# A hybrid encoder layer in split fp32: order of the loads at the turn to the down projection, a fixed list of down units, stores on another engine's queue

## The chip, the cores and the metric

The kernel runs on one NeuronCore of a Trainium2 chip. The metric is the device time of one execution in microseconds. Three runs of the kernel before took 2485.86 to 2487.36 us, with a median of 2487.01. One execution was taken by the hardware profiler; its own time was 2484.48 us, its span from the first instruction to the last 2482.8 us, with a mean granted TensorE clock of 0.987. All times of instructions below come from that one execution, counted from the start of its span.

## What is computed

One layer of a streaming encoder, in fp32, on 512 prompt frames and 64 sample frames (576 together), width D = 2048:

```python
def hybrid_layer(x, k_past, v_past, conv_past, g_norm1, w_in, g_q, g_k, conv_w,
                 g_attn_out, g_conv_out, w_out, g_norm2, w_gate, w_up, w_down):
    hn = rmsnorm(x, g_norm1)
    proj = hn @ w_in
    ...
    mix = jnp.concatenate([rmsnorm(o_attn, g_attn_out), rmsnorm(o_conv, g_conv_out)], axis=-1)
    x = x + mix @ w_out
    h2 = rmsnorm(x, g_norm2)
    x = x + (jax.nn.silu(h2 @ w_gate) * (h2 @ w_up)) @ w_down
    return x, k, v, new_conv
```

Eight heads of stick-breaking attention and eight groups of a short gated convolution make `mix`. The change touches only the last part, the feed-forward block: gate and up are 2048 x 5632, down is 5632 x 2048.

## The kernel before

**Split fp32.** Each operand is a pair: `hi`, the value rounded to fp32r by a ScalarE cast (L221), and `lo`, the rest, by a VectorE subtraction (L222). A product is three matmuls per 128 rows of depth, hi x hi, lo x hi and hi x lo, each over 288 columns, half of the frames (`step` L211, `multiply` L1067 to L1074).

**Stages.** In order: x is loaded, normed and turned; the input projection and the heads and groups run (to about 930 us with the output projection); the first 256 hidden channels ("pair 0" of 22 pairs) go through `wide`, the plain form, until 982 us; then 21 pairs, each a gate and an up unit, until 1927 us; then the down phase to the end. A spawned worker, `frame_sums`, makes the sums of frame halves (`tsum`) that the units need, beside the matmuls of `wide`.

**Units.** A unit computes a 256-wide block of outputs for all frames by seven products in place of eight, a Strassen-like form. The products are named 1, 2, 6, 7, 5, 3, 4 in the order in which a unit runs them, and (n, p) is product p of unit n. Operands of weights are sums and differences of the unit's two weight blocks: `prepare` makes them on VectorE and splits them two products ahead (`AHEAD = 2`), into four rotating buffers `whl`. Product 6 is the first that needs the unit's second block (the sum `s` at L1057). A gate or up unit has a depth of 8 steps of 256, so each product is 24 matmuls. The order of TensorE's products is a list written out by hand, `order`. It interleaves neighbours: the next unit's product 1 comes between a unit's products 5 and 3. The other engines' order follows from a scheduler.

**Forms.** The down phase needs seven combinations of each pair's hidden values. As the up unit ends, `put_forms` makes them, and `put_form` (L924 to L928) splits each one into a tile "hl" of two buffers and stores it, 288 KB, to DRAM. A store has to be done before the buffer's next cast.

**Down phase.** A unit (d, a, b) adds the pairs a to b - 1 to output block d, of eight. Its products are b - a steps deep, three matmuls each. `down_windows` computes the list of 35 units: 2, 3, 4, 5, 6 pairs at first, then mostly 6, with units of 1 to 3 at the end. A pair's seven forms come back as one 2016 KB slot; there are seven slots (`load_pair`, L1142 to L1146), three of which lie over the tiles of normed frames, and four, with everything else of the pool `dpool`, over the frame sums `tsum`. A slot is reloaded when all eight blocks have used its pair: `calls` says after which unit. For each unit the residual block x2, 576 KB, is loaded into one of two buffers (L1131), VectorE adds the products to it (L1140), and it is stored again (L1135) or, when the block is complete, turned and put out as y (L1161, L1162, L1168).

**Queues.** All these loads and stores are issued by SyncE (SP), which goes through its list in order: an instruction that waits holds up all behind it. At the turn the seven slots come first, each waiting for the tile that it lies over, then x2 of the first down unit, with the last pair's form stores between them.

Of the kernel before, what the change touches and what calls it, by code (L numbers as in the profile page):

```python
# [10 lines left out]
F32 = mybir.dt.float32  # L11
# [5 lines left out]
P = 128  # L17
# [3 lines left out]
HALF = T // 2  # L21
# [14 lines left out]
NFP = NFF // 2  # L36
DC = D // 256
SLOTS = 7
WINDOW = 6
FORMS = 7  # L40


def down_windows():

    done, units, calls, gone, turn = [0] * DC, [], [], {}, 0  # L50
    while min(done) < NFP:
        u = len(units)
        d = turn % DC
        turn += 1
        end = 0
        while end < NFP and (end < SLOTS or gone.get(end - SLOTS, u) <= u - 2):
            end += 1
        end = min(end, done[d] + WINDOW, u + 2 if u < DC else NFP)
        if end == done[d]:
            continue  # L60
        units.append((d, done[d], end))
        done[d] = end
        calls.append([p + SLOTS for p in range(min(done)) if p not in gone and p + SLOTS < NFP])
        for p in range(min(done)):
            gone.setdefault(p, u)
    return units, calls


class Pipeline:
# [28 lines left out]
def tile_hybrid_stream_step(  # L98
# [6 lines left out]
    nc = tc.nc  # L105
# [14 lines left out]
    tmp = ctx.enter_context(tc.tile_pool(name="tmp", bufs=2, side="left"))  # L120
    acon = tc.alloc_tile_pool(name="acon", bufs=1, side="left")
    xt_dram = tc.dram_tile([KD, P, T], F32, name="xt_dram")
    x2_dram = tc.dram_tile([KD, P, T], F32, name="x2_dram")
    hid_dram = tc.dram_tile([NFP, P, FORMS, 2, HALF], F32, name="hid_dram")
# [22 lines left out]

    UNITS = [(kind, fp, 0, NP) for fp in range(1, NFP) for kind in ("gate", "up")]
    NGU = len(UNITS)
    windows, calls = down_windows()  # L150
    UNITS += [("down", d, a, b - a) for d, a, b in windows]
    first_block = len(specs)
    for kind, i, a, n in UNITS:
        w = {"gate": w_gate, "up": w_up, "down": w_down}[kind]
# [54 lines left out]
    pipe = Pipeline()  # L209
# [10 lines left out]
    def split(hi, lo, src, lo_eng=None):  # L220
        nc.scalar.copy(out=hi, in_=src)  # L221
        (lo_eng or nc.vector).tensor_tensor(out=lo, in0=src, in1=hi.bitcast(F32), op=ALU.subtract)  # L222
# [141 lines left out]
    with tc.manual_schedule(engines={mybir.EngineType.Activation, mybir.EngineType.DVE, mybir.EngineType.SP}):  # L364
# [26 lines left out]
        for kt in range(KD + LAG):  # L391
# [19 lines left out]
            if kt in (14, 16):  # L411
                a = (kt - 14) * 512
# [424 lines left out]
    h2pool = tc.alloc_tile_pool(name="h2pool", bufs=1, reuse_waits="tile", side="left")  # L837
# [4 lines left out]
    b12pool = tc.alloc_tile_pool(name="b12pool", bufs=1, reuse_waits="tile", side="left")  # L842
# [44 lines left out]
    turn = [0]  # L887
# [9 lines left out]
    def frame_sums():  # L897

        for j in range(NP):
            ev, od = x2(2 * j), x2(2 * j + 1)  # L900
            ge, go = col("g2", 2 * j), col("g2", 2 * j + 1)
            pool, tag = (tpool, f"t{j}") if j < 4 else (ypool, f"y{j - 4}")
            b11 = tmp.tile([P, HALF], F32, tag="ms", name="b11", bufs=1)
            b22 = tmp.tile([P, HALF], F32, tag="t", name="b22", bufs=1)
            nc.scalar.activation(out=b11, in_=ev[:, :HALF], func=AF.Copy, scale=ge)
            nc.scalar.activation(out=b22, in_=od[:, HALF:], func=AF.Copy, scale=go)
            t1 = h2pool.tile([P, HALF], F32, bufs=2, tag="hx", name="t1")
            t2 = tmp.tile([P, HALF], F32, tag="sq", name="t2")
            t3 = h2pool.tile([P, HALF], F32, bufs=2, tag="hx", name="t3")
            t4 = tmp.tile([P, HALF], F32, tag="sq", name="t4")  # L910
            nc.vector.scalar_tensor_tensor(out=t1, in0=ev[:, HALF:], scalar=ge, in1=b11, op0=ALU.mult, op1=ALU.subtract)
            nc.vector.tensor_tensor(out=t2, in0=b22, in1=t1, op=ALU.subtract)
            nc.vector.scalar_tensor_tensor(out=t3, in0=ev[:, HALF:], scalar=ge, in1=b22, op0=ALU.mult, op1=ALU.subtract)
            nc.vector.scalar_tensor_tensor(out=t4, in0=od[:, :HALF], scalar=go, in1=t2, op0=ALU.mult, op1=ALU.subtract)
            tt = pool.tile([P, 2, 4, HALF], F32R, tag=tag, name=f"tsum{j}")
            for n, t in enumerate((t1, t2, t3, t4)):
                split(tt[:, 0, n, :], tt[:, 1, n, :], t)
            tsum.append(tt)
            yield 9

# [3 lines left out]
    def put_form(fp, n, src):  # L924

        t = tmp.tile([P, 2, HALF], F32R, tag="hl", name="form")
        split(t[:, 0], t[:, 1], src)
        nc.sync.dma_start(out=hid_dram[fp][:, n - 1], in_=t.bitcast(F32))  # L928

    def put_forms(fp, c, i):  # L930

# [42 lines left out]
    def wide(kind, hold=None):  # L974

        pss = {}
        for kk in range(2):
# [13 lines left out]
            if hold and kk == 0:  # L991
                hold()

    pipe.spawn(frame_sums(), 28)
    wide("gate", row_scale2)
    load_weight()
    wide("up")
# [21 lines left out]
        return [(tsum[j][:, 0, q, :], tsum[j][:, 1, q, :]) for j in range(m)]  # L1019

    NU = len(UNITS)
    order = [(0, 1), (0, 2), (0, 6), (0, 7), (0, 5)]
    for n in range(NU):
        if n == NGU - 1:

            order += [(n, 3), (n, 4), (n + 1, 1), (n + 1, 2), (n + 1, 6), (n + 1, 7), (n + 1, 5)]
            continue
        if n + 1 < NU:
            order.append((n + 1, 1))
        if n == NGU - 2:  # L1030
            order += [(n, 3), (n + 1, 2), (n + 1, 6), (n + 1, 7), (n + 1, 5), (n, 4)]
            continue
        order += [(n, 3), (n, 4)]
        if n + 1 < NU:
            order += [(n + 1, p_) for p_ in (2, 6, 7, 5)]
# [89 lines left out]
    xt2 = {}  # L1125
    down = {}

    def load_x2(n):
        d = UNITS[n][1]
        xt2[n] = down["pool"].tile([P, 2, T], F32, tag="x2", name=f"x2_{n}", bufs=2)  # L1130
        nc.sync.dma_start(out=xt2[n], in_=x2_dram[2 * d : 2 * d + 2].rearrange("k p t -> p k t"))  # L1131

    def store_x2(n):
        d = UNITS[n][1]
        nc.sync.dma_start(out=x2_dram[2 * d : 2 * d + 2].rearrange("k p t -> p k t"), in_=xt2.pop(n))  # L1135

    def add(n, c, i, src):
        a, b = HALVES[i]
# [3 lines left out]
    def load_pair(p):  # L1142
        tag = ("h2ah", "h2al", "b22", "s3", "s4", "s5", "s6")[p % SLOTS]
        pool = h2pool if p % SLOTS < 3 else down["pool"]
        slots[p] = pool.tile([P, FORMS, 2, HALF], F32R, tag=tag, name=f"slot{p}")
        nc.sync.dma_start(out=slots[p].bitcast(F32), in_=hid_dram[p])  # L1146
# [28 lines left out]
    for k_, (n, p_) in enumerate(order):  # L1175
        if p_ == 1:
            while len(raws) < min(first_block + 2 * (n + 1) + 2, len(specs)):
                load_weight()
        if (n, p_) == (NGU, 1):
            tpool.release()  # L1180
            ypool.release()
            down["pool"] = tc.alloc_tile_pool(name="dpool", bufs=1, reuse_waits="tile", side="right")
            for p in range(SLOTS):
                load_pair(p)
        if n >= NGU and p_ == 1:
            load_x2(n)
        if k_ + AHEAD < len(order):
            prepare(*order[k_ + AHEAD])
        run(n, p_)
        if n >= NGU and p_ == 4:  # L1190
            for p in calls[n - NGU]:
                load_pair(p)
# [35 lines left out]
```

## Time and profile before

| what | us |
|---|---|
| median of three runs | 2487.01 |
| profiled execution | 2484.48 |
| its span | 2482.8 |
| TensorE busy | 2422.5 |
| VectorE busy | 1759.9 |
| ScalarE busy | 1071.3 |
| GpSimd (POOL) busy | 118.3 |

How to read the profile: PE is TensorE's matmuls, PEld its weight loads beside them, DVE is VectorE, ACT ScalarE, POOL GpSimd; SPq, ACTq and PEq are what an engine's sequencer does, DMA issues above all. In a row of the timeline stand the start, the duration, the engine, the line of the kernel, the operation, and its tiles (out<-in, buffer numbers left out), with the number of instructions merged into the row. In brackets at the end is the idle time of the engine before the row, and what ended it. The granted clock (PEclk) is a share of full speed. The issue of a DMA is short; "to landing" is the time from there until the data has arrived. Tiles have short names there: the residual block x2 is x.

### The profile page before, as it was taken

How to read it: one execution, taken by the hardware profiler on the slowest of the kernel's cores; microseconds unless marked ns; L12 is line 12 of the kernel's file. 1: busy time of each engine (PE TensorE's matmuls, PEld its weight loads, DVE VectorE, ACT ScalarE, POOL GpSimd, SP SyncE). 2: the span in 40 equal slices, each digit the busy share in tenths (PEclk: the TensorE clock that was granted, in tenths of full speed). 3: DMA queues.
4: the chain of work that ended last, by engine and by line, in shares of the span. 5: the costliest groups of instructions: out<-in, count | busy, mean ns of one | idle time of the engine just before them, and what ended most of it. 6: DMA issues, size and time to landing. Idle time of an engine off the chain costs nothing.

```text
span 2482.8 us, 43866 instructions
## 1 busy us (share of the span) xinstructions
PE 2422.5 (98%) x18121; PEld 2411.9 (97%) x18121; DVE 1759.9 (71%) x2770; ACT 1071.3 (43%) x1869; POOL 118.3 (5%) x211
## 2 busy tenths in 40 slices
PE   8999999999999999999999999999999599999998
PEld 8999999999999999999999999999999599999998
DVE  7766666353335458888888888888887587777787
ACT  6655555231132345444444444444444343433443
POOL 2111010110020120000000000000000000000000
PEclk9999999999999999999999999999999799999998
DMA  8233322233242333435444454444454958778674
GB/s 268 82 93 87 91 76 84 81 88 86 78 155 84 105 123 122 135 118 159 145 143 138 126 155 150 137 137 133 150 155 156 321 173 276 246 254 264 214 215 133
DMA packets 465984, 368.33 MB, mean 148 GB/s; under 512 B 9790, under 2 KB 420024, under 8 KB 462968
## 3 DMA queue, kind: packets, MB, share of 16 engines
q1 hardware_dynamic: 464504, 365.01, 47.2%
q8 instruction: 142, 2.33, 0.4%
q10 hardware_dynamic: 1280, 0.53, 0.1%
q14 instruction: 58, 0.48, 0.1%
HBM read 285.26 MB, written 80.23 MB: 147 GB/s over the span
## 4 chain that ended last, share of the span: by engine, by line
PE 92%; DVE 3%; DMA 3%; ACT 1%; issue 0%; SPq 0%; ACTq 0%; DVEq 0%
PE psy L1071 32%; PE pj L213 23%; PE psw L1071 16%; PE pjo L213 8%; PE psx L1071 8%; DMA slot<-hid_dram 1%; DMA x<-x_dram 1%; DVE xlo L347 1%; PE z L551 1%; PE pw L986 1%; PE po L617 1%; DVE tsum L222 0%; PE os L647 0%; PE zs L577 0%; PE pot L1160 0%
## 5 line engine op out<-in xcount | busy, mean ns | idle before, releaser
L222 DVE TENSOR_TENSOR whl<-raw,whl 128x1024 fp32r<-128x1024 f32 (+5 forms) x462 | 481.2, 1042 | 109.4 <-ACT whl L221 108.3
L221 ACT CAST whl<-raw 128x1024 fp32r<-128x1024 f32 (+5 forms) x462 | 418.7, 907 | 299.4 <-issue 111.7
L213 PE MATMUL pj<-xhi,whi 128*128 128x288 f32 x1504 | 451.0, 300 | 0.0
L213 PE MATMUL pj<-xlo,whi 128*128 128x288 f32 x1504 | 445.2, 296 | 2.2 <-DVE xlo L347 2.2
L213 PE MATMUL pj<-xhi,wlo 128*128 128x288 f32 x1504 | 444.9, 296 | 0.0
L1071 PE MATMUL psy<-slot,whl 128*128 128x288 f32 x2112 | 299.6, 298 | 12.5 <-DMA slot<-hid_dram 9.8
L1071 PEld LDWEIGHTS psy<-slot,whl 128*128 128x128 f32 x2112 | 287.9, 190 | 14.3 <-DMA slot<-hid_dram 10.5
L1071 PE MATMUL psy<-tsum,whl 128*128 128x288 f32 x2016 | 283.8, 297 | 6.6 <-ACT whl L221 5.7
L213 PEld LDWEIGHTS pj<-xlo,whi 128*128 128x128 f32 x1504 | 284.5, 189 | 2.4 <-DVE xlo L347 2.4
L213 PEld LDWEIGHTS pj<-xhi,wlo 128*128 128x128 f32 x1504 | 284.9, 189 | 0.5 <-DVE wlo L177 0.2
L213 PEld LDWEIGHTS pj<-xhi,whi 128*128 128x128 f32 x1504 | 284.9, 189 | 0.3
L1071 PEld LDWEIGHTS psy<-tsum,whl 128*128 128x128 f32 x2016 | 274.4, 190 | 7.2 <-ACT whl L221 5.9
L1071 PE MATMUL psw<-tsum,whl 128*128 128x288 f32 x2016 | 280.9, 295 | 0.0
L1071 PEld LDWEIGHTS psw<-tsum,whl 128*128 128x128 f32 x2016 | 271.8, 189 | 0.0
L176 ACT CAST whi<-raw 128x1024 fp32r<-128x1024 f32 (+1 forms) x138 | 140.0, 1030 | 234.0 <-PE pj L213 95.8
L1081 ACT COPY part<-psy 128x288 f32<-128x288 f32 x231 | 92.1, 399 | 323.7 <-PE psy L1071 303.6
L1071 PE MATMUL psw<-slot,whl 128*128 128x288 f32 x1056 | 155.6, 299 | 25.0 <-DVE x L1140 25.0
L177 DVE TENSOR_TENSOR wlo<-raw,whi 128x1024 fp32r<-128x1024 f32 (+1 forms) x132 | 160.2, 1227 | 23.4 <-ACT whi L176 21.9
L1071 PEld LDWEIGHTS psw<-slot,whl 128*128 128x128 f32 x1056 | 146.6, 192 | 25.3 <-DVE x L1140 25.2
L1071 PE MATMUL psy<-b,whl 128*128 128x288 f32 x1008 | 140.2, 295 | 0.0
L1071 PEld LDWEIGHTS psy<-b,whl 128*128 128x128 f32 x1008 | 135.9, 188 | 0.0
L1071 PE MATMUL psy<-h2ah,whl 128*128 128x288 f32 x672 | 135.6, 296 | 0.0
(329 smaller groups left out, 3985.9 us busy)
## 6 DMA issues: line engine op xcount, KB each, us to landing
raw<-in_w_in_dram SPq DMA_DIRECT2D x47, 1024.0 KB, 5.5
raw<-in_w_gate_dram SPq DMA_DIRECT2D x44, 1024.0 KB, 6.2
raw<-in_w_up_dram SPq DMA_DIRECT2D x44, 1024.0 KB, 6.5
hid_dram<-form SPq DMA_DIRECT2D x154, 288.0 KB, 3.2
slot<-hid_dram SPq DMA_DIRECT2D x22, 2016.0 KB, 9.5
raw<-in_w_down_dram SPq DMA_DIRECT2D x40, 768.0 KB, 5.9
x<-x_dram SPq DMA_DIRECT2D x35, 576.0 KB, 4.6
raw<-in_w_out_dram SPq DMA_DIRECT2D x16, 1024.0 KB, 5.3
```

The source lines that it names most:

```text
L176: nc.scalar.copy(out=hi[:, a:b], in_=raw[:, a:b])
L177: lo_eng.tensor_tensor(out=lo[:, a:b], in0=raw[:, a:b], in1=hi[:, a:b].bitcast(F32), op=ALU.subtract)
L213: mm(ps, w_[:, k, csl], x_[:, k, a:b], start=(k == 0 and n == 0), stop=(k == nk - 1 and n == 2))
L221: nc.scalar.copy(out=hi, in_=src)
L222: (lo_eng or nc.vector).tensor_tensor(out=lo, in0=src, in1=hi.bitcast(F32), op=ALU.subtract)
L347: nc.vector.scalar_tensor_tensor(out=xlo[:, kt, :], in0=st, scalar=g1c[:, kt : kt + 1], in1=xhi[:, kt, :].bitcast(F32), op0=ALU.mult, op1= ...
L551: mm(zb[i], a_[:, kk], b_[:, q0:TP], start=(n == 0), stop=False, skip_group_check=True)
L617: mm(po[:, i * P : 512], a_[:, i, :], b_[:, : 512 - i * P], stop=(i == 0 and n == 2), **kw)
L986: mm(pss[j, i], w_[:, k, j * P : (j + 1) * P], x_, start=(kk == 0 and k == 0 and n == 0), stop=(kk == 1 and k == 7 and n == 2))
L1071: mm(ps, whl[:, w_, j, :], x_, start=(start and j == 0 and q == 0), stop=(j == len(xs_) - 1 and q == 2), skip_group_check=True)
L1081: nc.scalar.copy(out=t, in_=st["y"])
```

## The change

- The first units' order: product 1 of the second unit comes before product 6 of the first, and the second unit's product 2 before the first's 3.
- The down units are a fixed list, `DOWN`: 36 units of 3 to 7 pairs. The number of pairs and blocks, and so of matmuls, stays.
- At the turn only three slots are issued ahead of the first residual block; slot 3 follows it, and slots 4 to 6 follow one per unit, behind that unit's residual block.
- The stores of forms and of residual blocks are issued by GpSimd.
- `frame_sums` writes the four sums into one tile and splits them with one cast and one subtraction of 1152 columns; its worker starts after 20 ticks in place of 28.

In the changed program SP has 403 instructions (495 before), and POOL 154 form stores and 28 stores of residual blocks.

```diff
-WINDOW = 6
+DOWN = (
+    (0, 0, 3), (1, 0, 4), (2, 0, 4), (3, 0, 4), (4, 0, 5), (0, 3, 7), (5, 0, 4), (6, 0, 5), (7, 0, 6),
+    (1, 4, 7), (2, 4, 8), (3, 4, 8), (4, 5, 10), (5, 4, 9), (6, 5, 10), (0, 7, 12), (7, 6, 11), (1, 7, 12),
+    (5, 9, 14), (2, 8, 15), (3, 8, 15), (4, 10, 15), (6, 10, 15), (7, 11, 16), (0, 12, 17), (1, 12, 15),
+    (5, 14, 19), (1, 15, 19), (2, 15, 22), (1, 19, 22), (3, 15, 22), (4, 15, 22), (5, 19, 22), (6, 15, 22),
+    (0, 17, 22), (7, 16, 22),
+)
+def down_calls():
+    done, calls, gone = [0] * DC, [], 0
+    for d, a, b in DOWN:
+        assert done[d] == a and b <= gone + SLOTS
+        done[d] = b
+        calls.append([p + SLOTS for p in range(gone, min(done)) if p + SLOTS < NFP])
+        gone = min(done)
...
-            t1 = h2pool.tile([P, HALF], F32, bufs=2, tag="hx", name="t1")
...
+            t = b12pool.tile([P, 4, HALF], F32, tag="ht", name="t")
+            t1, t2, t3, t4 = (t[:, n] for n in range(4))
...
-            for n, t in enumerate((t1, t2, t3, t4)):
-                split(tt[:, 0, n, :], tt[:, 1, n, :], t)
+            split(tt[:, 0], tt[:, 1], t)
...
-        nc.sync.dma_start(out=hid_dram[fp][:, n - 1], in_=t.bitcast(F32))
+        nc.gpsimd.dma_start(out=hid_dram[fp][:, n - 1], in_=t.bitcast(F32))
...
-    pipe.spawn(frame_sums(), 28)
+    pipe.spawn(frame_sums(), 20)
...
-    order = [(0, 1), (0, 2), (0, 6), (0, 7), (0, 5)]
-    for n in range(NU):
+    order = [(0, 1), (0, 2), (1, 1), (0, 6), (0, 7), (0, 5), (1, 2), (0, 3), (0, 4), (1, 6), (1, 7), (1, 5)]
+    for n in range(1, NU):
...
-        nc.sync.dma_start(out=x2_dram[2 * d : 2 * d + 2].rearrange("k p t -> p k t"), in_=xt2.pop(n))
+        nc.gpsimd.dma_start(out=x2_dram[2 * d : 2 * d + 2].rearrange("k p t -> p k t"), in_=xt2.pop(n))
...
-            for p in range(SLOTS):
+            for p in range(3):
                 load_pair(p)
-        if n >= NGU and p_ == 1:
             load_x2(n)
+            load_pair(3)
+        if n > NGU and p_ == 1:
+            load_x2(n)
+            if n < NGU + SLOTS - 3:
+                load_pair(n - NGU + 3)
```

More of the change, by code (lines that the diff above doesn't have):

```diff
@@ L38 @@
 SLOTS = 7
-WINDOW = 6
 FORMS = 7
[L43 to L66, printed above, removed]
+DOWN = (
[5 rows of a table added]
+)
[6 more added lines that the diff above has]
+        gone = min(done)
+    assert gone == NFP
+    return calls
 class Pipeline:
@@ L149, in tile_hybrid_stream_step @@
     NGU = len(UNITS)
-    windows, calls = down_windows()
-    UNITS += [("down", d, a, b - a) for d, a, b in windows]
+    calls = down_calls()
+    UNITS += [("down", d, a, b - a) for d, a, b in DOWN]
     first_block = len(specs)
@@ L906, in frame_sums @@
             nc.scalar.activation(out=b22, in_=od[:, HALF:], func=AF.Copy, scale=go)
-            t1 = h2pool.tile([P, HALF], F32, bufs=2, tag="hx", name="t1")
-            t2 = tmp.tile([P, HALF], F32, tag="sq", name="t2")
-            t3 = h2pool.tile([P, HALF], F32, bufs=2, tag="hx", name="t3")
-            t4 = tmp.tile([P, HALF], F32, tag="sq", name="t4")
+            t = b12pool.tile([P, 4, HALF], F32, tag="ht", name="t")
+            t1, t2, t3, t4 = (t[:, n] for n in range(4))
             nc.vector.scalar_tensor_tensor(out=t1, in0=ev[:, HALF:], scalar=ge, in1=b11, op0=ALU.mult, op1=ALU.subtract)
```

## The prediction

> **What bounds the kernel now.** I read the page's totals first, then the share of each engine in the chain that ended last, then windows of TensorE to find where it stands, and then the timeline of each such place.
>
> ```profile
> span 2482.8 us, 43866 instructions
> ...
> PE 2422.5 (98%) x18121; PEld 2411.9 (97%) x18121; DVE 1759.9 (71%) x2770; ACT 1071.3 (43%) x1869; POOL 118.3 (5%) x211
> ...
> PE 92%; DVE 3%; DMA 3%; ACT 1%; issue 0%; SPq 0%; ACTq 0%; DVEq 0%
> ```
>
> TensorE is busy for 98% of the span. The change touches no matmul, so it can win only what TensorE now loses: idle time, and time at a lower clock. The windows show where that is (columns: window, us, PE busy with its matmuls, granted clock, DMA share, GB/s).
>
> ```profile
> 980.00:1000.00 20.00, 13.37 (x84) 0.78 0.69 209
> 996.00:1000.00 4.00, 3.93 (x16) 0.50 0.38 147
> 1920.00:1940.00 20.00, 13.50 (x100) 0.92 1.01 388
> 1940.00:1960.00 20.00, 0.00 (x0) 0.50 0.99 382
> 1960.00:1980.00 20.00, 19.05 (x132) 0.90 0.72 228
> 1980.00:2000.00 20.00, 20.00 (x152) 1.00 0.76 221
> 2060.00:2080.00 20.00, 16.11 (x121) 1.00 0.95 321
> 2080.00:2100.00 20.00, 20.00 (x142) 0.91 0.92 286
> 2220.00:2240.00 20.00, 16.61 (x106) 0.83 0.98 330
> 2460.00:2480.00 20.00, 14.95 (x81) 0.73 0.37 97
> ```
>
> A full window holds 152 matmuls, so one matmul of 288 columns costs 20/152 = 0.1316 us. Missing matmuls times 0.1316 is the loss, and that counts idle time and low clock together. By that measure:
> - The step into the first gate/up units (980 to 1000) misses 68: 8.9 us.
> - The turn to the down phase (1920 to 1980) misses 52 + 152 + 20 = 224: 29.5 us.
> - Three later windows of the down phase miss 31 + 10 + 46 = 87: 11.4 us.
> - The tail, 2460 to the end at 2482.8, holds some 81 matmuls in 22.8 us: 22.8 - 10.7 = 12.1 us.
>
> Together 62 us. Each part of the change aims at one of the four.
>
> **The first units.**
>
> ```profile
> 968.02 0.37 SPq L183 DMA_DIRECT2D raw<-in_w_up_dram  x1
> ...
> 982.30 0.37 SPq L183 DMA_DIRECT2D raw<-in_w_gate_dram  x1
> ...
> 988.65 1.23 DVE L1057 TENSOR_TENSOR s<-raw 128x1024 f32<-128x1024 f32 x1 [3.25 <-DMA raw<-in_w_gate_dram]
> ...
> 994.51 0.61 PE L1071 MATMUL psy<-tsum,whl 128*128 128x288 f32 x1 [5.68 <-ACT whl L221]
> ```
>
> Product (0,6) needs sums of the unit's second weight block, and that load is issued at 982.30 and read at 988.65. TensorE stands 5.68 us before it, and the window 996 to 1000 then runs at a clock of 0.50. The changed order puts (1,1) there: 8 pairs x 3 = 24 matmuls = 3.2 us of work whose block was loaded at 968.02. It moves work and adds none, so it covers 3.2 us; the idle stretch left is about 2.5 us, and a part of the low-clock stretch goes too. What is late next is (0,6)'s own cast on ScalarE: in the changed order seven casts of pair 0's forms stand before it (five now), over two buffers. With a store that takes L us to free its buffer the seventh ends near 984 + 3L, at L = 3.5 near 994.5, and the operand near 995.6; (0,6) then starts at about the time it starts now, with 3.2 us done already. I take a loss of 5.4 in place of 8.9: **-3.5 us**. Ends: -7 (nothing late) and +3 (L at the 7.4 of a row below).
>
> The frames' sums become one 1152-wide cast and one subtraction in place of four each: the same elements, fewer starts.
>
> ```profile
> L221 ACT CAST tsum<-t x32: 415/428/435, 934.5 to 978.1; 128x288 fp32r<-128x288 f32 x32
> ```
>
> The last cast ends at 978 and the first reader of tsum is the matmul at 994.51. That cover of some 14 us hides it: **0**. If the one group buffer serialised the groups, it would have to lose those 14 us before anybody waited.
>
> **The turn.**
>
> ```profile
> 1924.10 0.32 SPq L1146 DMA_DIRECT2D slot<-hid_dram  x1
> ...
> 1936.76 1.16 SPq L928 DMA_DIRECT2D hid_dram<-form  x2
> 1938.01 0.41 SPq L1146 DMA_DIRECT2D slot<-hid_dram  x1
> 1942.40 0.32 SPq L928 DMA_DIRECT2D hid_dram<-form  x1
> 1942.82 0.89 SPq L1146 DMA_DIRECT2D slot<-hid_dram  x2
> 1943.80 0.44 SPq L1131 DMA_DIRECT2D x<-x_dram  x1
> ...
> 1923.90 3.32 PE L1071 MATMUL psw<-tsum,whl 128*128 128x288 f32 x24
> ...
> 1934.51 1.47 PE L1071 MATMUL psy<-slot,whl 128*128 128x288 f32 x9 [2.48 <-DMA slot<-hid_dram]
> ...
> 1960.95 1.33 PE L1071 MATMUL psw<-slot,whl 128*128 128x288 f32 x4 [24.98 <-DVE x L1140]
> ```
>
> SP issues in order. The residual tile x of unit 0 stands behind seven slots and behind form stores that themselves wait for ScalarE, so it goes out only at 1943.80, and then shares the engines with 2016 KB slots at 382 GB/s. VectorE can't add, the accumulators stay full, and TensorE stands 24.98 us.
>
> After the change the form stores are POOL's, and SP goes slot 0, 1, 2, x(0), slot 3. Slot 2 is still freed when (up,3) ends, at 1924.10.
>
> ```profile
> DMA to landing us min/median/max: 10.4/10.4/10.4
> ```
>
> That is slot 2's landing, and 1924.10 + 10.4 = 1934.5, which the matmul at 1934.51 confirms. Unit 0 now has three pairs and so can't start on two as now: TensorE idles from the end of the last up product, 1923.90 + 3.32 = 1927.2, to 1934.5, 7.3 us; then come about 4 us at half clock. In the window 996 to 1000, 16 matmuls stand where 30 would fit, which is 1.9 us lost. Loss 9.2. Behind it: x(0), issued near 1927.3, and slot 3 right after it, since both lie over sums whose last reader ends there. Slot 3 at 10.4 and some sharing lands by about 1941.4, and it is wanted by unit 1 after the first five products of unit 0, 5 x 9 = 45 matmuls = 5.9 us plus 1.9 behind 1934.5, at 1942.3. So it holds by one microsecond. Slots 4 to 6 go out one per unit, each unit being 7 products of 4 pairs = 84 matmuls = 11 us, against 9.5 per slot. The loss goes from 29.5 to 9.2: **-20.3 us** (ends -22.2, if the clock doesn't drop, and -12, the first rival).
>
> **The fixed list.**
>
> ```profile
> hid_dram<-form SPq DMA_DIRECT2D x154, 288.0 KB, 3.2
> slot<-hid_dram SPq DMA_DIRECT2D x22, 2016.0 KB, 9.5
> ```
>
> ```profile
> 2078.89 3.68 PE L1071 MATMUL psy<-slot,whl 128*128 128x288 f32 x18 [3.88 <-DMA slot<-hid_dram]
> ```
>
> Later losses are waits for slots, as at 2078.89. A slot is reloaded when the last of the eight output blocks has used its pair. I counted for each reloaded pair the products between that and the first unit that reads it, at 3 x 0.1316 = 0.395 us per pair. Pair 0 is free at the first of six steps of the last product of (7,0,6), and pair 7 is read in the fourth step of (2,4,8): 5 + 4 products x 3 + 3 = 20 steps lie between, 7.9 us against 9.5 landing. All other pairs have 10.4 us or more. So 1.6 us of wait are left, and about 0.4 for units of three pairs, whose seven products of 1.2 us leave VectorE little room. Loss 2 in place of 11.4: **-9.4 us** (ends -11.4 and -4, the latter if landings stretch to 12 or 13 us next to weight loads).
>
> **The tail.**
>
> ```profile
> 2474.61 0.73 PE psw L1071 x3
> ...
> 2479.24 0.56 DVE ob L1161
> ```
>
> The last product ends at 2475.3 and the span at 2482.8. That part (adds, transposes, copy, the last store) is unchanged. Before it, one- and two-pair units leave gaps; the last two units are now 5 and 6 pairs. I take 7 of the 12.1 us as staying: **-5 us** (ends -6.6 and -2).
>
> **The stores on POOL.** 154 form stores and 28 x stores leave SP. The trace has no POOL DMA, so its cost is bounded by the nearest rows. The cast of the third form waits for the store of the first:
>
> ```profile
> 1395.55 0.45 DVE L222 TENSOR_TENSOR form<-ut,form 128x288 fp32r<-128x288 f32 x1
> ...
> 1398.22 0.43 ACT L221 CAST form<-ut 128x288 fp32r<-128x288 f32 x1 [0.57 <-DMA hid_dram<-form]
> 1398.53 0.45 DVE L222 TENSOR_TENSOR form<-ux,form 128x288 fp32r<-128x288 f32 x1
> ...
> 1402.54 0.40 ACT L1081 COPY part<-psy 128x288 f32<-128x288 f32 x1 [0.47 <-PE psy L1071]
> ```
>
> ```profile
> L865 POOL TENSOR_TENSOR acc<-acc,sq 128x288 f32<-128x288 f32 x30 | 26.3, 875 | 175.9 <-ACT sq L864 175.9
> ```
>
> ```profile
> x_dram<-x SPq DMA_DIRECT2D x27, 576.0 KB, 7.4
> ```
>
> From the end of the subtraction (1396.00) to the cast (1398.22) is L = 2.2 us on SP, the lower end. The upper end is 7.4, an x store behind the loads of its ring. I take 3.5: 2.2, plus one POOL instruction of 0.875, near the 3.2 of form stores as a whole. Behind a cast that waits are ScalarE's next operand cast and its copy of a partial product, and TensorE waits for that copy only when the accumulator is wanted again:
>
> ```profile
> 1405.70 9.58 PE psy L1071 x72
> ```
>
> The third form's subtraction ends at 1398.98; the cast that waits for its store (0.43), and the copy of (n,6)'s partial product that follows it in the changed order (0.40), have to be done by 1405.70, when the next product into that accumulator starts, so the cast by 1404.8. So the cover per pair is 5.8 us: at L = 3.5 the 21 pairs cost **0**; above 5.8 each us costs 21 pairs + 3 (first units) + 2 (turn) = 26 us.
>
> The Trainium skill, page "DMA: Bandwidth & Descriptors", section "Anatomy of one DMA", gives a POOL-issued DMA 2.0 us plus bytes/436e3; by it a form store would take an estimated 2.7 us, and the sum would come out the same, with 0.8 us x 3 = 2.4 us less at the first units. No run here shows it yet.
>
> **The sum.** -3.5 - 20.3 + 0 - 9.4 - 5 + 0 = -38 us. The profiled execution took 2484.5 us (span 2482.8), so 2446.3 on its basis. The median of the runs is 2487.0, 2.5 above, so 2448.8; I forecast **2449 us**.
>
> **Rivals.**
> 1. *Transfers bound the turn and the list anyway.* For: the DMA share is 1.01 and 0.99 from 1920 to 1960. If slots 0 to 3 and x(0) shared one stream, slot 2 would come 5 us later (2016 KB at 382 GB/s is 5.4 us), slot 3 and x(0) too, and the turn would lose 17.5 (-12), the list win 4, and the rest stay: -3.5 - 12 - 4 - 5 = -24.5, **2462 us**. Against: slot 2 is issued before slot 3 and x(0) may go, at 1927, so little else is in flight.
> 2. *POOL's stores gate ScalarE: slower.* Place: the two form buffers, in each of 21 pairs. It decides from L = 5.8, and eats the gain of 38 at 5.8 + 38/26 = 7.3. Near the 7.4 of x stores, with the casts queued for two stores in a row (a form store behind another on POOL), L reaches 7.7: 26 x 1.9 = 49, **2498 us**. For: POOL executes the stores one after another, and four come in about 5 us. Against: POOL is busy 5%, and its ring holds no loads. The Trainium skill, page "SBUF — State Buffer", box "The 'DVE blocks DMA' trap" in "SBUF: two separate sides", speaks for this rival: GpSimd writes a DMA's descriptors and is locked out while VectorE runs in a two-port mode. Its section "Who interferes with whom" says that tensor_tensor has no such mode, and VectorE's rows here are those; no run here shows the lock.
> 3. *The change does not do what it says*: loads still wait on something other than SP's order. Then the turn keeps 29.5 and the list changes both ways: **2485 us**. Against: slot 4 and x went out right behind form stores on SP (1936.76 to 1938.01, 1942.40 to 1943.80), so the order did hold them.
>
> **How the numbers follow.** Forecast 0.58 (own range 2438 to 2460), rival 1 with halves of it 0.24 (to 2474), rival 2 0.12, rival 3 0.04, below 2438 0.02. The range 2438 to 2474 leaves out 0.18. A difference of 0.2%, 5 us, is about what a measurement can tell from none. Faster by more: 0.85 (forecast, rival 1, below, a little of 3); within: 0.03; slower: 0.12 (rival 2).
>
> **What would show it.** TensorE's longest wait (24.98 for x) should be gone, and one of about 7 us for slot 2 stand in its place. The window of the first units should miss some 40 matmuls, not 68. Slot waits later in the down phase should sum to about 2 us. ScalarE's form casts may wait longer for stores, while TensorE shows no wait for part copies. The prediction is wrong if POOL's form stores land after more than 5.8 us, if slot 2 or slot 3 lands after more than 12, or if units of three pairs leave TensorE waiting for VectorE's adds each time.

## The result, and the profile after

The changed kernel takes 2492.31 us (median of 20 runs, 2486.31 to 2498.02), the kernel before 2486.89 us (20 runs, 2481.87 to 2491.35): a ratio of 1.0023 with a 95% interval of 1.0016 to 1.0031. It is slower by some 5 us, where 38 us of gain were forecast. The profiled execution took 2492.62 us.

The page of the changed kernel, totals and the chain that ended last:

```profile
span 2490.9 us, 43942 instructions
...
PE 2427.2 (97%) x18121; PEld 2414.4 (97%) x18121; DVE 1757.3 (71%) x2764; ACT 1069.6 (43%) x1855; POOL 222.2 (9%) x393
...
PE 53%; issue 35%; DMA 4%; POOL 3%; DVE 3%; ACT 1%; SPq 0%; POOLq 0%; ACTq 0%; DVEq 0%
```

TensorE executes the same 18121 matmuls. The share of "issue" in the chain is new. It is time for which the chain shows no releaser, and TensorE's busy time says that it is mostly no loss. The windows tell more. These are TensorE's windows of the changed kernel, with the columns and at the places of those before:

```profile
980.00:1000.00 20.00, 12.73 (x93) 0.88 0.65 206
996.00:1000.00 4.00, 0.61 (x1) 0.50 0.38 147
1920.00:1940.00 20.00, 12.18 (x80) 0.84 0.98 382
1940.00:1960.00 20.00, 14.81 (x92) 0.73 0.63 225
1960.00:1980.00 20.00, 20.00 (x152) 1.00 1.01 340
2060.00:2080.00 20.00, 11.44 (x84) 0.84 1.01 409
2080.00:2100.00 20.00, 17.77 (x114) 0.82 0.74 234
2220.00:2240.00 20.00, 20.00 (x153) 1.00 0.52 155
```

The empty window of the turn (1940 to 1960) now holds 92 matmuls. But 2060 to 2100 misses 106 where it missed 41, and more such places follow. Two of them are 2160 to 2200 and 2320 to 2360:

```profile
2160.00:2180.00 20.00, 18.77 (x137) 1.00 0.84 265
2180.00:2200.00 20.00, 15.96 (x117) 1.00 0.86 297
2320.00:2340.00 20.00, 13.89 (x103) 0.91 1.05 382
2340.00:2360.00 20.00, 19.28 (x124) 0.83 0.48 152
```

They ran at full rate in the kernel before; its second and third of these windows:

```profile
2180.00:2200.00 20.00, 20.00 (x153) 1.00 0.54 162
2320.00:2340.00 20.00, 20.00 (x153) 1.00 0.59 173
```

What TensorE waited for in the changed kernel (engine, line and releaser; us in total, times, longest):

```profile
PE psy L1064 <- ACT whl L217: 16.9, 2, 10.5
PE psy L1064 <- DMA slot<-hid_dram: 14.2, 3, 7.0
PE psy L1064 <- ACT part L1074: 6.7, 3, 6.0
PE psy L1064 <- DVE whl L218: 6.5, 6, 3.2
```

The wait of 25 us for the residual block is gone, as forecast. In its place stand weight operands (whl), slots, and a partial product's copy.

**A measure for all runs.** The loss of a stretch is its length less its matmuls at 20/152.7 = 0.131 us. It has a floor: from 1100 to 1900 in the kernel before TensorE is busy throughout at a clock of 1.00 with 6040 matmuls, and the measure still gives 8.9 us. So only differences between kernels are read. The stretch 1980 to 2360 is counted in one piece here; the expectations counted it in six windows, which take some matmuls twice at the edges (36.8 where it is 38.0 here, 14.5 where it is 16.0). All values come from one profiled execution each, so small differences say little. Each ratio is to runs of the kernel before in the same rounds, with medians of 2486.65 to 2488.34. "End" is 2360 to the last instruction.

| kernel | median us | ratio to before, 95% | first units 980–1020 | turn 1920–1980 | list 1980–2360 | end |
|---|---|---|---|---|---|---|
| before | 2486.89 | | 9.9 | 29.6 | 16.0 | 14.9 |
| changed | 2492.31 | 1.0016–1.0031 | 10.7 | 17.8 | 38.0 | 11.8 |
| e1_old_list | 2470.22 | 0.9918–0.9947 | 10.3 | 16.5 | 14.4 | 14.6 |
| e2_stores_sp | 2476.91 | 0.9937–0.9970 | 7.3 | 14.2 | 31.9 | 11.5 |
| e3_turn_seven_first | 2501.49 | 1.0038–1.0068 | 11.2 | 27.5 | 35.6 | 11.7 |
| e4_spread | 2488.38 | 0.9995–1.0014 | 11.1 | 15.5 | 33.4 | 12.0 |
| e5_forms_sp | 2484.08 | 0.9979–0.9999 | 7.5 | 14.6 | 38.5 | 11.5 |
| e6_old_list_sp | 2470.49 | 0.9916–0.9946 | 6.9 | 15.5 | 17.3 | 14.6 |
| e7_before_turn | 2473.19 | 0.9928–0.9958 | 9.6 | 17.0 | 17.8 | 14.5 |
| e8_hl3 | 2488.82 | 0.9997–1.0015 | 10.7 | 10.9 | 41.1 | 14.3 |
| e9_old_sums | 2493.54 | 1.0010–1.0034 | 12.5 | 17.4 | 38.4 | 11.6 |
| e10_part_reload | 2466.88 | 0.9902–0.9932 | 10.3 | 16.9 | 14.0 | 9.1 |
| e11_before_list | 2493.37 | 1.0011–1.0031 | 10.0 | 29.1 | 28.4 | 12.4 |
| e12_best | 2481.17 | 0.9966–0.9985 | 6.9 | 13.1 | 16.5 | 27.7 |
| e13_room | 2469.91 | 0.9910–0.9949 | 6.7 | 16.5 | 16.9 | 15.3 |
| e14_x2_pool | 2486.35 | 0.9985–1.0004 | 10.9 | 15.5 | 31.7 | 15.3 |
| e15_tail | 2466.24 | 0.9906–0.9936 | 6.6 | 16.3 | 16.5 | 15.6 |

The changed kernel's row against the one before: +0.8, -11.8, +22.0 and -3.1, together +7.9, against 8.1 between the spans. Most of the lost gain is in the list.

**At the first burst.** The timeline of the changed kernel on SP, ScalarE and TensorE, from the ninth down unit (7, 0, 6):

```profile
2054.01 2.13 SPq L1139 DMA_DIRECT2D slot<-hid_dram  x4
2059.92 16.41 SPq L179 DMA_DIRECT2D raw<-in_w_down_dram  x2
2076.42 3.53 SPq L1124 DMA_DIRECT2D x<-x_dram  x1
...
2081.44 1.66 ACT L217 CAST whl<-raw 128x512 fp32r<-128x512 f32 x3 [9.44 <-DMA raw<-in_w_down_dram]
...
2082.11 6.06 PE L1064 MATMUL psy<-slot,whl 128*128 128x288 f32 x24 [10.54 <-ACT whl L217]
```

And the time to landing: of the fourth slot, the only one of the four for which the view gives it, then of the two weight loads behind them:

```profile
DMA to landing us min/median/max: 24.7/24.7/24.7
...
DMA to landing us min/median/max: 21.5/21.9/22.4
```

With (7, 0, 6), the first unit of the last block, four pairs at once have been used by all eight blocks; the list of before frees two there. Four slots go out in 2 us: 8 MB, some 22 us at the 382 GB/s of the turn's empty window before. The weight blocks of the next units stand behind them and land after 22 us; the median of the changed kernel's 16 loads of that size, 512 KB, is 6.0. ScalarE waits 9.4 us for them and TensorE 10.5 for ScalarE.

### The profile page after: what moved, and what is told of

Same layout as the page of the kernel before. It is cut to its first block, busy times and chain, and to the rows that moved or that the text cites. A ratio compares the mean times of both kernels' runs of the same rounds, so it can differ in the third digit from the quotient of the medians.

```text
span 2490.9 us, 43942 instructions
## 1 busy us (share of the span) xinstructions
PE 2427.2 (97%) x18121; PEld 2414.4 (97%) x18121; DVE 1757.3 (71%) x2764; ACT 1069.6 (43%) x1855; POOL 222.2 (9%) x393
## 4 chain that ended last, share of the span: by engine, by line
PE 53%; issue 35%; DMA 4%; POOL 3%; DVE 3%; ACT 1%; SPq 0%; POOLq 0%; ACTq 0%; DVEq 0%
PE pj L209 23%; PE psy L1064 10%; PE pjo L209 8%; PE psw L1064 5%; POOL hid_dram L921 3%; PE psx L1064 2%; DMA raw<-in_w_down_dram 2%; DMA slot<-hid_dram 1%; DMA hid_dram<-form 1%; PE z L547 1%; PE pw L979 1%; PE po L613 1%; DVE whl L218 0%; PE os L643 0%; PE zs L573 0%
## 5 line engine op out<-in xcount | busy, mean ns | idle before, releaser
L1064 PE MATMUL psy<-slot,whl 128*128 128x288 f32 x2112 | 307.3, 301 | 37.1 <-DMA slot<-hid_dram 14.2
L1064 PEld LDWEIGHTS psy<-slot,whl 128*128 128x128 f32 x2112 | 292.9, 193 | 40.8 <-DMA slot<-hid_dram 15.3
L921 POOL DMA_DIRECT2D hid_dram<-form x154 | 83.5, 542 | 928.6 <-DVE form L218 764.7
## 6 DMA issues: line engine op xcount, KB each, us to landing
slot<-hid_dram SPq DMA_DIRECT2D x22, 2016.0 KB, 10.9
```

Source lines behind the costliest of these rows:

```text
L921: nc.gpsimd.dma_start(out=hid_dram[fp][:, n - 1], in_=t.bitcast(F32))
L1064: mm(ps, whl[:, w_, j, :], x_, start=(start and j == 0 and q == 0), stop=(j == len(xs_) - 1 and q == 2), skip_group_check=True)
```

## The experiments

Theories at the start: **burst** (the list sends slots out together, and weight loads queue behind them), **queue** (residual loads on SP wait for GpSimd's stores and hold what is behind), and **store** (forms' stores gate ScalarE at the two turns).

### e1: the old list

The changed kernel with `DOWN` replaced by the 35 units of before:

```diff
-    (0, 0, 3), (1, 0, 4), (2, 0, 4), (3, 0, 4), (4, 0, 5), (0, 3, 7), (5, 0, 4), ...
+    (0, 0, 2), (1, 0, 3), (2, 0, 4), (3, 0, 5), (4, 0, 6), (5, 0, 6), (6, 0, 6), (7, 0, 6), (0, 2, 7), ...
```

> The changed kernel with the list of down units of before (35 units, two to six pairs, slots released at most two at a time); all else as changed. Burst theory (the fixed list frees four slots at once at its ninth unit and two at once later, their 2016 KB loads go out together and the weight loads behind them on the same queue land late): the losses of the down phase behind the turn fall from some 37 us to the 11 us of before, and the small last units cost 3 to 4 us more: 2466 to 2474 us. Queue theory (residual loads on SP wait for stores that GpSimd issues, and hold the weight loads): the list does not matter, 2486 to 2494 us. Store theory (forms' stores gate ScalarE at the two turns): also 2486 to 2494 us.

Measured: 2470.22 us. The list alone costs 22 us within the changed kernel. The window of the list (e1_old_list, TensorE):

```profile
1980.00:2360.00 380.00, 374.04 (x2791) 0.99 0.75 244
```

2791 matmuls where the changed kernel fits 2611. The end loses 14.6 as it did before: the 3 us won there belong to the list.

### e2 and e5: stores on SP

```diff
-        nc.gpsimd.dma_start(out=hid_dram[fp][:, n - 1], in_=t.bitcast(F32))
+        nc.sync.dma_start(out=hid_dram[fp][:, n - 1], in_=t.bitcast(F32))
...
-        nc.gpsimd.dma_start(out=x2_dram[2 * d : 2 * d + 2].rearrange("k p t -> p k t"), in_=xt2.pop(n))
+        nc.sync.dma_start(out=x2_dram[2 * d : 2 * d + 2].rearrange("k p t -> p k t"), in_=xt2.pop(n))
```

> The changed kernel with forms' and residual blocks' stores issued by SP again. Burst theory: the down phase behind the turn is as in the changed kernel; at the turn slot 3 and the residual block stand behind forms' stores again, 0 to +8 us: 2492 to 2500 us. Queue theory: the waits for weights go away, 2475 to 2482 us. Store theory: TensorE's 6.0 us wait for a copy at the turn shortens or goes and the first units win 3 to 4 us: 2483 to 2488 us.

Measured: 2476.91 us, 15 us less than the changed kernel. The time lies in the queue theory's range, but that theory had only a part of the gain: the profile shows 6.1 us less loss in the list, and 3.4 at the first units and 3.6 at the turn, where the store theory had put it. e5 has only the first of the two edits:

> The changed kernel with the forms' stores on SP again and the residual blocks' stores left on GpSimd. With both on SP the first units lost 7.3 us in place of 10.7, the turn 14.2 in place of 17.8, and the stretch 2110 to 2220 2.7 in place of 9.6. If the forms' stores are behind the first two, those gains (7 us) show here and the third does not: 2483 to 2487 us. If forms' stores are behind all three: 2475 to 2479 us. If the residual blocks' stores are behind it: 2489 to 2494 us.

Measured: 2484.08 us: the forms' stores cost 8 us, of which the profile shows 3.2 at the first units and 3.2 at the turn. The other 7 us come with the residual blocks' stores.

### e3: seven slots first

```diff
-            for p in range(3):
+            for p in range(SLOTS):
                 load_pair(p)
-            load_x2(n)
-            load_pair(3)
-        if n > NGU and p_ == 1:
+        if n >= NGU and p_ == 1:
             load_x2(n)
-            if n < NGU + SLOTS - 3:
-                load_pair(n - NGU + 3)
```

> The changed kernel with the seven slots ahead of the first residual block again; stores stay on GpSimd. If the order of the loads is what shortened the turn, the first residual block lands some 4 slots later (4 x 5.4 us), the turn loses about 28 us in place of 17, and the time is 2500 to 2506 us. If taking forms' stores off SP is what shortened it, the time stays at 2490 to 2495 us.

Measured: 2501.49 us, and the turn loses 27.5. It is the order of the loads that shortens the turn, not that the stores left SP: those are on GpSimd here too.

### e4: the same list, slots spread

After each unit one released slot is loaded, more only where the unit after next needs them:

```diff
-            for p in calls[n - NGU]:
-                load_pair(p)
+            waiting += calls[n - NGU]
+            need = max((UNITS[u][2] + UNITS[u][3] for u in range(n + 1, min(n + 3, NU))), default=0)
+            first = True
+            while waiting and (first or waiting[0] < need):
+                load_pair(waiting.pop(0))
+                first = False
```

> The changed kernel with released slots loaded one per unit, more only where the unit after next needs them; the list stays. Burst theory: the 10.5 us wait for a weight cast at the first burst and its half-clock stretch go, and half of the later ones: 2474 to 2481 us. If the list asks for more bandwidth than there is at that place, or the queue or store theory holds: 2488 to 2495 us.

Measured: 2488.38 us, at the edge of the upper range expected. In 2050 to 2110 the loss falls from 14.4 to 6.6, but 2110 to 2170 gets 2.6 worse and 2300 to 2360 stays at 11.8 (11.3). So the burst in its narrow sense, issue in one go, is the smaller part. The open question was then whether the list fails by bytes or by something else that it carries.

### e10: fewer bytes on each reload

A reloaded slot gets only forms 1 to 4 of its pair. What this leaves out: products 5 to 7 of those pairs read the old pair's forms, so the outputs y are not the reference's.

```diff
+        if p < SLOTS:
             slots[p] = pool.tile([P, FORMS, 2, HALF], F32R, tag=tag, name=f"slot{p}")
             nc.sync.dma_start(out=slots[p].bitcast(F32), in_=hid_dram[p])
+        else:
+            slots[p] = slots[p - SLOTS]
+            nc.sync.dma_start(out=slots[p][:, :4].bitcast(F32), in_=hid_dram[p][:, :4])
```

> The changed kernel, but a slot that is reloaded gets only forms 1 to 4 of its pair, 1152 KB in place of 2016 (its products 5 to 7 read the old pair's forms, so the output is not the reference's). The list, the leads, the releases and the order of issue stay. If the fixed list loses by bytes that are due in too short a time, with weight loads queued behind them, the losses from 1980 to 2360 fall from 36.8 us to 10 to 16, 2466 to 2474 us. If it loses by the fixed delay from a release to a landing, or by the waits on stores: 2486 to 2493 us.

Measured: 2466.88 us. TensorE's windows, first of e10_part_reload, then of the changed kernel:

```profile
1980.00:2360.00 380.00, 374.90 (x2794) 1.00 0.74 235
```

```profile
1980.00:2360.00 380.00, 356.40 (x2611) 0.96 0.76 256
```

With the same list, the same order and the same releases, 864 KB less per reload take 24 of the 38 us away. At the first burst the four slots still go out within 2 us (from 2053.25), but the fourth lands after 14.4 us in place of 24.7, and the two weight loads behind it after 12.4 and 14.6. The loss is in the bytes that are due in too short a time. The mean DMA share of the two is nearly the same, 0.74 and 0.76: a mean over the stretch does not show it.

### e6 and e11: how list and stores go together

e6 has the old list and all stores on SP; e11 is the kernel before with nothing but the new list.

```diff
-    windows, calls = down_windows()
+    calls = down_calls()
+    windows = DOWN
```

> The list of before and both stores on SP, with the changed order of first units, sums and loads at the turn. If the list (-22 us) and the stores (-15 us) are separate costs: 2455 to 2461 us. If they are one cost seen twice (the same late weight loads): 2468 to 2472 us.

> The kernel before with only the fixed list of down units. If the list costs by itself what it cost in the changed kernel (22 us, some 36 us lost between 1980 and 2360 in place of 14, 3 back at the tail): 2503 to 2511 us. If it costs only together with GpSimd's stores: 2482 to 2492 us.

Measured: 2470.49 and 2493.37 us. With the old list it makes no difference to the time who issues the stores (2470.22 and 2470.49): of 4.4 us won at the first units and the turn, the list gives 2.9 back. With the new list it is 15 us. Put the other way, the list costs 22 us with stores on GpSimd, and 6.4 (e2 against e6) or about 5 (e11 against before) with stores on SP. The expectation for e11, 2503 to 2511, was wrong: list and stores don't add, they share a cost.

### e14: residual loads off SP

Where they share it is seen in SP's own waits from 1980 to 2360, first of the changed kernel, then of e2_stores_sp:

```profile
SPq L1124 <- DMA x_dram<-x: 176.1, 22, 13.8
```

```profile
SPq L1128 <- DVE x L1133: 92.1, 23, 9.6
...
SPq L1124 <- DMA x_dram<-x: 42.7, 18, 4.8
```

And in the order on SP, around one unit's residual load (2155.66 in the first, 2145.72 in the second), again the changed kernel and then e2_stores_sp:

```profile
2155.66 0.37 SPq L1124 DMA_DIRECT2D x<-x_dram  x1
2156.12 1.09 SPq L179 DMA_DIRECT2D raw<-in_w_down_dram  x2
2165.95 0.37 SPq L1124 DMA_DIRECT2D x<-x_dram  x1
2169.24 1.47 SPq L179 DMA_DIRECT2D raw<-in_w_down_dram  x2
```

```profile
2143.28 1.67 SPq L179 DMA_DIRECT2D raw<-in_w_down_dram  x2
2145.72 2.07 SPq L1124 DMA_DIRECT2D x<-x_dram  x1
2151.89 0.37 SPq L1128 DMA_DIRECT2D x_dram<-x  x1
```

The residual block's load waits until an earlier store has freed its buffer. With stores on GpSimd the scheduler puts that load ahead of two weight loads that it follows with stores on SP. By SP's timelines this is so at nine of the 36 units, four of them between 2110 and 2220. e14 takes the waiting load off SP:

```diff
-        nc.sync.dma_start(out=xt2[n], in_=x2_dram[...])
+        (nc.gpsimd if n > NGU + 6 else nc.sync).dma_start(out=xt2[n], in_=x2_dram[...])
```

> The changed kernel with the residual blocks' loads, from the eighth down unit on, issued by GpSimd, behind the stores that they wait for. Queue theory (on SP the residual block's load stands ahead of weight loads and waits for a store that GpSimd has issued, 176 us in all): the stretch 2110 to 2220 loses 2 to 4 us in place of 9.6, 2482 to 2487 us, most of what both stores on SP won there. If the extra loss came from transfers of GpSimd's queue sharing the DMA engines with the slots: 2490 to 2495 us.

Measured: 2486.35 us. TensorE's windows of the stretch in question, first of e14_x2_pool, then of the changed kernel:

```profile
2110.00:2220.00 110.00, 110.00 (x827) 1.00 0.82 261
```

```profile
2110.00:2220.00 110.00, 104.38 (x765) 0.98 0.76 245
```

The loss there falls from 9.8 us to 1.7 although more bytes move (261 against 245 GB/s). So it was the order on SP, not the sharing of DMA engines. The time falls by 6 us: 8 are won in this stretch and 2 at the turn, and the first burst and the end lose some more than in the changed kernel.

### e8 and e9: a third form buffer

In the changed kernel the group's tile "ht" takes the room, so e9 gives up the joint split of sums (its worker starts after 28 ticks again), and e8 adds a buffer for forms (and gives up one of two output buffers, "ob").

```diff
-            split(tt[:, 0], tt[:, 1], t)
+            for n, t in enumerate((t1, t2, t3, t4)):
+                split(tt[:, 0, n, :], tt[:, 1, n, :], t)
...
-            ob = down["pool"].tile([P, 3, P], F32, tag="ob", name="ob", bufs=2)[:, : b1 - b0]
+            ob = down["pool"].tile([P, 3, P], F32, tag="ob", name="ob", bufs=1)[:, : b1 - b0]
...
+        nform[0] += 1
+        t = (tmp if nform[0] % 3 < 2 else h2pool).tile([P, 2, HALF], F32R, ...)
-        t = tmp.tile([P, 2, HALF], F32R, tag="hl", name="form")
```

> The changed kernel with the sums of frames split one at a time again, from four tiles, started after 28 ticks. Off the path, as predicted: 2490 to 2495 us, the first units lose 10 to 11 us as in the changed kernel. If the 1152-wide split delays the first pair's forms and with them the first units: 2486 to 2489 us.

> As the run with the sums split one at a time, and a third buffer for forms (one of the two output buffers of the last stage is given up for its room). If a form's cast that waits for its store is what holds ScalarE, and TensorE behind it, at the two turns: first units 4 to 6 us in place of 10.7, the turn 10 to 13 in place of 17.8, 2478 to 2485 us. If the waits for stores are covered and something else holds TensorE there: as that other run.

Measured: 2493.54 and 2488.82 us. The joint split is worth nothing in the time (2492.31 and 2493.54), as forecast. The third buffer takes the turn from 17.4 to 10.9 and the first units from 12.5 to 10.7, so a form's cast that waits for its store does hold TensorE there; 4 to 6 was expected for the first units, and there something else is left. The time stayed above the expected 2478 to 2485: the list lost 41.1 in place of 38.4, and the end 14.3 in place of 11.6. The latter fits the lost output buffer; the former was not looked into.

### e7, e12, e13, e15: towards a faster kernel

e7 is the kernel before with only the order of loads at the turn:

```diff
-            for p in range(SLOTS):
+            for p in range(3):
                 load_pair(p)
-        if n >= NGU and p_ == 1:
             load_x2(n)
+            load_pair(3)
+        if n > NGU and p_ == 1:
+            load_x2(n)
+            if n < NGU + SLOTS - 3:
+                load_pair(n - NGU + 3)
```

> The kernel before with only the order of loads at the turn changed (three slots, the residual block, slot 3, then one per unit). If the order alone wins the turn: from 29.6 us lost to 14 to 18, 2470 to 2475 us. If forms' stores on SP hold the residual block whatever the order: 2484 to 2488 us.

Measured: 2473.19 us, a ratio of 0.9943. This one edit holds most of what the change had to give: with everything but the list the ratio is 0.9932 (e1).

e12 is e6 with the sums of before, the third form buffer and a single output buffer; e13 takes the output buffers from the form buffers' room:

```diff
-            ob = down["pool"].tile([P, 3, P], F32, tag="ob", name="ob", bufs=2)[:, : b1 - b0]
+            ob = tmp.tile([P, 2, HALF], F32, tag="hl", name="ob").rearrange("p a b -> p (a b)")[:, : (b1 - b0) * P] ...
```

> List and sums of before, all stores on SP, changed order of first units and of loads at the turn, and a third buffer for forms. The run without that buffer took 2470.5 us and the third buffer took 6.5 us off the turn: 2461 to 2466 us. If on SP's queue the form buffers are not what holds the turn: 2468 to 2473 us.

> As the run with list and sums of before, all stores on SP and a third form buffer, but with both output buffers of the last stage kept (they use the room of the form buffers, which are free by then). That run lost 27.6 us in its last two windows against 14.7 without the third form buffer. If giving up the output buffer is what lost it: 2465 to 2470 us, and 2470.5 without the third form buffer says what that buffer wins. If the third form buffer itself disturbs the end: 2476 to 2482 us.

Measured: 2481.17 and 2469.91 us; e12 lies above both of its ranges. The output buffer was worth 12 us at the end (27.7 against 15.3), and the third form buffer wins nothing when stores are on SP and the old list stands (2469.91 against 2470.49).

e15 is e13 with the last seven units in the order 4, 3, 4, 2, 4, 1, 4:

```diff
-    (4, 18, 22), (5, 18, 22), (6, 18, 22), (7, 18, 22), (0, 19, 22), (1, 20, 22), (2, 21, 22),
+    (4, 18, 22), (0, 19, 22), (5, 18, 22), (1, 20, 22), (6, 18, 22), (2, 21, 22), (7, 18, 22),
```

> As the first of these, with the last seven units of the old list in the order of pairs 4, 3, 4, 2, 4, 1, 4 in place of 4, 4, 4, 4, 3, 2, 1: no burst is added. If the tail of before is lost because VectorE and the weight splits can't keep up with units of 3, 2 and 1 pairs in a row, the last two windows lose 10 to 12 us in place of 14.7: 2462 to 2467 us. If small units cost the same wherever they stand: as the first.

Measured: 2466.24 us, the fastest kernel here that computes the whole: 0.9906 to 0.9936 of before. Whether the tail's order did it is open. Its interval overlaps e13's, and its profiled execution, the slowest of its four runs (2470.92), loses 15.6 at the end, not the 10 to 12 expected.

## Why the prediction was wrong, point by point

**The fixed list: the step that failed.** The prediction gave it -9.4 us, with ends of -11.4 and -4; it was +22.0. It set each reloaded slot's lead against the landing of one slot, 9.5 us: "7.9 us against 9.5 landing" for pair 7, and "All other pairs have 10.4 us or more". It did not count that one unit's end frees pairs 0 to 3 together, so that 8 MB and the weight loads behind them share one stream. e1 shows that the list is the cause, e10 that it is by bytes. Pair 7 itself was nearly on time. It is the first of the four slots, issued at 2054.01, and a weight load of TensorE waited for it only briefly:

```profile
2062.10 1.63 PEld L1064 LDWEIGHTS psy<-slot,whl 128*128 128x128 f32 x12 [0.36 <-DMA slot<-hid_dram]
```

What TensorE waited for at 2082 was a weight. The lead was also counted as if a slot's load were issued when its pair is free. The longest wait for a slot in the list, for pair 21, shows that it need not be:

```profile
2325.30 4.03 SPq L1124 DMA_DIRECT2D x<-x_dram  x1
2329.42 0.44 SPq L1139 DMA_DIRECT2D slot<-hid_dram  x1
...
2340.72 3.97 PE L1064 MATMUL psy<-slot,whl 128*128 128x288 f32 x15 [6.30 <-DMA slot<-hid_dram]
```

The product that frees this slot ended at 2324.8. But SP, which goes through its list in order, stood at a residual load that waited until 2325.3 for a store issued by GpSimd and then took 4.03 us to issue. So the slot went out 4.6 us late and landed after 11.3 us, and TensorE stood 6.30 us.

**The stores on POOL.** Taken as free, with L = 3.5 us against a cover of 5.8. In the 21 gate/up pairs that held: the stretch 1020 to 1920 loses 10.2 us before and after. The row of the page for the changed kernel, then the view of tile form from 970 to 1005 (the first units) and from 1920 to 1955 (the turn):

```profile
hid_dram<-form POOLq DMA_DIRECT2D x154, 288.0 KB, 2.6
```

```profile
DMA to landing us min/median/max: 2.4/2.6/7.9
```

```profile
DMA to landing us min/median/max: 2.4/6.5/8.7
```

The median is 2.6. The Trainium skill's page "DMA: Bandwidth & Descriptors", section "Anatomy of one DMA", gave an estimated 2.7, and the trace agrees. The stores that count took longer. At the first units the three for which casts wait took 4.4 to 7.9 us, next to two weight loads, where on SP the stores took 3.6 to 3.9 (e2). At the turn it was 6.5 with up to 8.7, above the 5.8 from which the second rival decides. But there they land no sooner on SP (6.6 to 7.9 in e2), and single stores took up to 7.4 between 1400 and 1900 without a loss. So rival 2's mechanism, form casts that hold ScalarE, was right for the first units and the turn, 5 of the 26 us that it counted for each us of L; the 21 pairs, the rest, held. Stores and list together added what the prediction had no term for, the order on SP (e14).

**The turn.** Forecast 29.5 to 9.2; measured 29.6 to 17.8. TensorE's and ScalarE's timeline of the changed kernel there:

```profile
1935.91 1.09 PE L1064 MATMUL psy<-slot,whl 128*128 128x288 f32 x3 [6.97 <-DMA slot<-hid_dram]
...
1945.19 2.53 PE L1064 MATMUL psy<-slot,whl 128*128 128x288 f32 x9 [6.04 <-ACT part L1074]
...
1942.92 0.43 ACT L217 CAST form<-ux 128x288 fp32r<-128x288 f32 x1 [6.27 <-DMA hid_dram<-form]
...
1944.75 0.39 ACT L1074 COPY part<-psy 128x288 f32<-128x288 f32 x1
```

The first wait, 6.97 us for slot 2, is the 7.3 of the working. The second was not in it: the copy of a partial product stands on ScalarE behind form casts that wait for stores. e8 removes it with a third buffer. With the forms' stores on SP it is 0.35 us (e2), though they land no sooner. There the copy stands ahead of the last two form casts, at

```profile
1933.54 0.40 ACT L1074 COPY part<-psy 128x288 f32<-128x288 f32 x1
```

So the order on ScalarE, which also comes from the scheduler, has a part in it beside the landing; the runs do not separate the two. That the order of the loads is what wins the turn was right (e3, e7).

**The first units.** Forecast 8.9 to 5.4, measured 9.9 to 10.7 (the forecast's window ends at 1000; up to there 59 matmuls are missing in place of 68, and the rest of the loss comes after it). Product (1,1) covers its 3.2 us, but (0,6) then starts late. Its timeline in the changed kernel:

```profile
989.01 0.43 ACT L217 CAST form<-ut 128x288 fp32r<-128x288 f32 x1 [5.50 <-DMA hid_dram<-form]
...
998.45 0.61 PE L1064 MATMUL psy<-tsum,whl 128*128 128x288 f32 x1 [6.33 <-ACT whl L217]
```

The prediction had named this (the operand behind the form casts, ends of -7 and +3) and taken too small a landing: 3.5 us, where the stores in question took 4.4 to 7.9. With forms on SP the step gives 7.3 to 7.5 (e2, e5).

**The tail and the sums.** -5 forecast, -3.1 measured, and it is the list's (e1). The sums cost nothing, as forecast (e9).

**The rivals.** The first, transfers that stay the bound, named the right resource and priced it as a smaller gain (the list still winning 4); it was a loss. The range's upper end rested on that price.

## What to carry to other kernels

Set a transfer's lead against everything that is due in the same stretch, not against its own landing alone: add the bytes released together, and the loads that queue behind them, and divide by the rate of the trace. When a store moves to another engine's queue, look at what waits for its buffer and where a scheduler now puts that load: here a load that waited for it went ahead of weight loads on SP, and held up a slot's load. Of a change with several parts, run each alone: here one part held most of the gain, and two others cost it together.

## What the runs showed of the hardware

An issue on SP can itself take long, so the remark ahead of the prediction that an issue is short does not always hold. With four slots in flight, of the two weight issues at 2059.92 the first took 0.38 us and the second 15.53, where the pair at 2169.24 took 1.47 from first to last. Everything behind it on SP waits. It goes with the bytes in flight: with 1152 KB per slot (e10_part_reload) the two issues are

```profile
2059.16 5.96 SPq L179 DMA_DIRECT2D raw<-in_w_down_dram  x2
```

and where one slot goes out ahead of them (e4) they took 1.69. The profile's list of waits puts 9.7 us of the 15.53 down to a VectorE subtraction that ends at 2070.05. In e10 the same issue was over at 2065.1, before VectorE came to that subtraction (2068.21), so it does not wait for it. How much the queue takes before an issue stalls was not measured.

A store issued by GpSimd costs that engine little. The group of the page for the changed kernel:

```profile
L921 POOL DMA_DIRECT2D hid_dram<-form x154 | 83.5, 542 | 928.6 <-DVE form L218 764.7
```

These are 542 ns each in the mean and none over 769, while VectorE is busy 71% of the span; the lock of which the Trainium skill's page "SBUF — State Buffer" warns, in its box on the "DVE blocks DMA" trap, does not show in it.
